# A hybrid decoder block: the order of work around the two halves of the attention values

## The chip, the core and the metric

The kernel runs on one core of a Trainium2 chip. The core has a matrix engine (TensorE, "PE"; its weight loads are listed apart as "PEld"), a vector engine (VectorE, "DVE"), an activation engine (ScalarE, "ACT"), a general-purpose engine (GpSimd, "POOL") and a queue engine (SyncE, "SP") that issues most of the transfers. Each engine works through its own instructions in the order in which they were laid down, and waits on semaphores for the others. The metric is device time in microseconds (us) of one execution; the median of three runs before the change is 1088.16 us (1085.83 to 1088.22).

## The reference, cut to what matters

```python
xn = rmsnorm(h, norm_mix_g)
proj = xn @ w_in                      # 1024 tokens x 2568 columns
q, k, v = ...                         # 512 columns each, 8 heads of 64
log_f = log_sigmoid(proj[..., 2560:] + b_forget)       # 8 columns
att = forgetting_attention(q, k, v, log_f)             # logits + c_i - c_k, c = cumsum(log_f)
uv = gelu(proj[..., 1536:2560])       # u and vg, 512 columns each
vg = rmsnorm over groups of 64, times v_gain
sg = u * (tril(w_s) @ vg per chunk of 128 tokens + b_s)
h = h + concat(att, sg) @ w_out
h = h + conv_ffn(rmsnorm(h), w_up, conv_w, conv_b, w_down)
return rmsnorm(h, norm_final_g)
```

`rmsnorm` divides by the root of the mean square plus 1e-6. All arrays are float32. The projection `proj` is what the change is about; the attention, the output projection and the feed-forward part are left as they are.

## The kernel before, in words

**Arithmetic.** Every float32 operand of a large product is split into a high part (a cast to the fp32r type, mostly on ACT) and a low part (the difference, mostly on DVE), and each product is three matmuls (high times high, high times low, low times high). `split_w` (L152), `own` (L206), `hl_of` (L212) and `tsplit` (L246) do this. The weight splits go through a ring of six buffers (`ring`, tags `wy` x2 and `whl` x4). The products are done in a Strassen form: the input is cut into quarters (x11, x12, x21, x22), the weights into A11, A12, A21, A22; seven products with the operands B11, B21, T2, T3, T1, T4 and B22 replace eight. S1 to S4 are sums of weight quarters. A product is `tprod`/`tmul` (L253) where the tokens are the stationary side, `product` (L420) for queries and keys, 12 matmuls of 512 columns each.

**Stages before the attention, in program order.**

1. Loads (L221 to L242) on SP, in the order in which they are written: x11, x21, x12, the weights of the low value half `wl`, `wl3`, then x22, then the gate's remaining weights `gb`.
2. B11 and B21 products for the gate's `uv` columns; then `values_low(0..3)` (L287), the low half of the values, which also carries the 8 forget columns; between them `t2_of` makes the T2 operand and `hl_of("T2", j, ...)` splits it. From L271 to L316 ACT and DVE are held to the program's order by a chain (`Line.on`).
3. The T2, T3, T1, T4 and B22 products for `uv` (L330 to L395). `sum23(k)` makes the weight sums S3 and S2, `sum4(k)` makes S4, and L353 adds the halves of the `gb` tiles; all of these adds are on DVE. The token norm `rstd1` is made from `xtok` (L363 to L368). Gelu follows as the results come.
4. The upper half of the values (L397 to L407), 96 matmuls of 264 columns; its weights `wh` are loaded into `pt` tiles, the last two late. `keep` stores a half's result in DRAM, and keeps the forget columns in `zf`.
5. Queries and keys: `Weights(0)` (L458), `q1` and `q2`, the last gelu of `ut[1]`, `scale_row` (a PE transpose of `rstd1`, a DVE copy, a write and a broadcast read by ACT's queue, giving the row `rb`), then four steps `qk_step(i)`. Each has the products S2, S3, (A12), S1, A22, the next step's A11, and S4; `nxt_of(i)` does the next step's loads, splits and, on POOL, sums (L447 to L455). `emit` (L528) scales and splits a result and stores it.
6. Mixed into stage 5: `gate_part` (L539) squares and reduces the gate per group of 64 and, on the second call for a half, takes the root and multiplies: for the upper half ahead of step 0, for the lower half in steps 0 and 1. `forget_sums` (L492) makes the log-sigmoid, the four small matmuls with the triangle and the ones (L509, L510), the running sums, and returns `turn` (L517), which transposes and stores.
7. The second value quarters (L637 to L813): `VH` and `VL` are accumulated in PSUM banks from `w0` and `wvr`; `gate_split` (L643) splits the normed gate; `kept(hf)` (L666) reloads a stored half and evacuates it; then `spatial` (L704), chained again on ACT and DVE: it splits the spatial weights, evacuates all eight blocks of `VH` and `VL` with `evac_v`, and runs the eight groups of the spatial product, each in a PSUM bank that DVE and ACT then read.

**What sets the order.** Outside the chained parts a planner lays down each engine's order by its own estimate of when an instruction will be ready, with the program's order as priority; `after(later, earlier)` fixes the order of two instructions on one engine. Tiles with one tag share a fixed number of buffers (`BUFS`, L87: for example `pt` 3, `G` 4, `gg` 2, `t01` 1), so that a new tile waits until an old one's last reader is done.

Of the kernel before, what the change touches and what calls it, by code (L numbers as in the profile page):

```python
# [8 lines left out]
F32 = mybir.dt.float32  # L9
# [56 lines left out]
def block_kernel(ctx: ExitStack, tc: tile.TileContext, xT, xtok, wuv, wv0, wv1, wqk, cpk, bfv,  # L66
# [161 lines left out]
    for k in range(4):  # L228
        load_x("x12", k, k, 1)
    wl = sb("A", [P, 3, 2, 264])  # L230
# [5 lines left out]
    for k in range(4):  # L236
        load_x("x22", k, 4 + k, 1)
# [94 lines left out]
    for k in range(4):  # L332
        tmul(S, tsplit(s2[k]), "T2", k, True)
        sum4(k)
        if k < 2:
            sum23(k + 2)
# [15 lines left out]
    for w in gb:  # L352
        dve.tensor_tensor(out=w[:, 0, :], in0=w[:, 0, :], in1=w[:, 1, :], op=ALU.add)  # L353
# [14 lines left out]
    dve.reciprocal(rstd1, rstd1)  # L368

# [26 lines left out]

    S = [sbank() for _ in range(4)]  # L397
    for k in range(4):
        if k > 1:
            t = sb("pt", [P, 2, 264])  # L400
            sp.dma_start(out=t, in_=wv0[k])
            wh.append(t)
        t = wh[k]
        pool.tensor_tensor(out=t[:, 1, :], in0=t[:, 0, :], in1=t[:, 1, :], op=ALU.add)
        tmul(half(S), tsplit(t[:, 0, :], n=264), "T3", k, True)
        tmul(half(S), tsplit(t[:, 1, :], n=264), "B22", k, False)
    keep(S, 1)  # L407

    rb = sb("t01", [P, 1024])

    def scale_row():
        pst = sbank()
        pe.transpose(pst[0:8, 0:P], rstd1, ident)
        rbt = sb("pt", [8, P])
        dve.tensor_copy(rbt, pst[0:8, 0:P])
        act.dma_start(out=rbd, in_=rbt)
        act.dma_start(out=rb, in_=rbd.rearrange("a b -> (a b)").unsqueeze(0).to_broadcast((P, 1024)))

# [38 lines left out]

    W = [Weights(0)]  # L458
    W[0].split("A11", "A12")
    W[0].sums()  # L460
    W[0].last_sum()
    xu = {}
# [11 lines left out]
    for m in range(4):  # L474
# [1174 lines left out]
```

## Time and profile before

| quantity | value |
|---|---|
| median of three runs | 1088.16 us |
| the profiled execution, its own device time | 1087.45 us |
| its span in the trace | 1085.7 us |
| mean granted clock of PE | 0.993 |
| PE busy | 1054.0 us, 97% |
| DVE busy | 892.8 us, 82% |
| ACT busy | 570.7 us, 53% |
| POOL busy | 236.4 us, 22% |
| DMA, mean over the span | 143 GB/s |

The trace's views are read like this. The timeline lists instructions in order of time: start, duration, engine, line, operation, output and inputs by the program's names, a count where equal ones are merged, and in brackets the idle time before it with what ended it. Most lines of DVE and ACT read L44 or L51, which are the lines of the `Line` helper that records them; they are told apart by their tiles. The view by stretches gives each engine's busy time between two moments, then PE's granted clock, the DMA share and GB/s. Matmul ends are modelled, so a start is a better measure than a duration.

### The profile page before, as it was taken

Reading aid. Unit: us, or ns where it says so; the run is one execution under the profiler, and the core shown is the slowest. Engines: PE = TensorE matmul, PEld = TensorE weight load, DVE = VectorE, ACT = ScalarE, POOL = GpSimd, SP = SyncE. Lnnn points to the kernel's source line nnn. Section 1 sums busy time; section 2 is a strip of 40 time slices with the busy share of each in tenths; the row PEclk is TensorE's granted clock in tenths of the full one; section 3 lists DMA queues with packets and bytes.
Section 4 is the critical chain, followed back from the end, with each engine's and each line's share of the span. In section 5 each row is a group of like instructions: output and inputs, shape, how many; then the busy total and the mean of one; then the engine's idle time right before and its main releaser. Section 6 shows DMA issues by size and latency. Waiting matters only on the chain.

```text
span 1085.7 us, 14637 instructions
## 1 busy us (share of the span) xinstructions
PE 1054.0 (97%) x5157; PEld 884.1 (81%) x5157; DVE 892.8 (82%) x1301; ACT 570.7 (53%) x1015; POOL 236.4 (22%) x177
## 2 busy tenths in 40 slices
PE   9999799979999999999999999999999999999997
PEld 6878677868889888887888888888888888888886
DVE  6993698867778877999899998989988775898774
ACT  6656534545767674754344444445444444454653
POOL 0010243340122353035334333233332000000000
PEclk9999899999999999999999999999999999999999
DMA  9152156845564454322243523323231899433442
GB/s 332 52 185 77 59 137 166 210 153 152 176 180 146 137 194 141 112 98 97 78 165 119 176 95 126 116 68 127 97 107 40 281 329 319 136 98 97 136 127 96
DMA packets 66160, 155.78 MB, mean 143 GB/s; under 512 B 7996, under 2 KB 8724, under 8 KB 66088
## 3 DMA queue, kind: packets, MB, share of 16 engines
q1 hardware_dynamic: 65656, 154.30, 44.4%
q8 instruction: 40, 0.66, 0.3%
q10 hardware_dynamic: 432, 0.57, 0.2%
q14 instruction: 32, 0.26, 0.1%
HBM read 111.96 MB, written 42.87 MB: 143 GB/s over the span
## 4 chain that ended last, share of the span: by engine, by line
PE 74%; DVE 5%; ACT 1%; issue 1%; DMA 0%; DVEq 0%; ACTq 0%; SPq 0%
PE k L1499 19%; PE qa L1241 11%; PE qc L1241 10%; PE qd L1241 10%; PE qb L1241 5%; PE pb L938 3%; PE pb L919 2%; PE pl L879 2%; PE pl L880 2%; PE ps L259 1%; PE pf L963 1%; PE pf L965 1%; PE pf L964 1%; PE pb L1152 1%; PE pb L1151 1%
## 5 line engine op out<-in xcount | busy, mean ns | idle before, releaser
L1499 PE MATMUL k<-whb,wha 128*128 128x512 f32 x924 | 209.8, 389 | 0.0
L1499 PEld LDWEIGHTS k<-whb,wha 128*128 128x128 f32 x924 | 173.4, 188 | 36.2 <-DVE wha L161 0.2
L1241 PE MATMUL qc<-xT,whb 128*128 128x512 f32 x540 | 129.9, 389 | 0.5 <-DVE u L1352 0.5
L1241 PE MATMUL qa<-xB,wha 128*128 128x512 f32 x528 | 127.2, 390 | 0.0
L1241 PEld LDWEIGHTS qc<-xT,whb 128*128 128x128 f32 x540 | 101.2, 188 | 22.1 <-DVE u L1352 0.9
L1241 PEld LDWEIGHTS qa<-xB,wha 128*128 128x128 f32 x528 | 98.8, 188 | 20.8 <-DVE wha L161 0.4
L155 ACT CAST wha<-sg 128x512 fp32r<-128x512 f32 x77 | 47.8, 623 | 96.8 <-PE k L1499 86.2
L155 ACT CAST whb<-sg 128x512 fp32r<-128x512 f32 x82 | 50.5, 617 | 87.3 <-PE qc L1241 68.9
L161 DVE TENSOR_TENSOR wha<-sg,wha 128x512 fp32r<-128x512 f32 x77 | 52.8, 688 | 41.5 <-ACT wha L155 41.3
L920 ACT CAST pt<-pb 128x512 fp32r<-128x512 f32 (+1 forms) x80 | 42.2, 545 | 43.0 <-PE pb L919 34.4
L1241 PE MATMUL qd<-xB,whb 128*128 128x512 f32 x264 | 63.9, 390 | 0.1
L1241 PE MATMUL qd<-xT,whb 128*128 128x512 f32 x264 | 63.6, 389 | 0.0
L161 DVE TENSOR_TENSOR whb<-sg,whb 128x512 fp32r<-128x512 f32 x82 | 57.8, 705 | 4.4 <-ACT whb L155 4.3
L1241 PE MATMUL qb<-xT,whb 128*128 128x512 f32 x252 | 60.9, 389 | 0.0
L1128 POOL TENSOR_TENSOR sg<-raw 128x512 f32<-128x512 f32 x20 | 30.4, 1518 | 136.1 <-DVE whb L161 79.9
L921 DVE TENSOR_TENSOR pt<-pb,pt 128x512 fp32r<-128x512 f32 (+1 forms) x80 | 48.8, 634 | 12.0 <-ACT pt L920 10.9
L1241 PEld LDWEIGHTS qd<-xB,whb 128*128 128x128 f32 x264 | 49.5, 188 | 10.8 <-DVE h L1360 0.5
L1241 PEld LDWEIGHTS qd<-xT,whb 128*128 128x128 f32 x264 | 49.6, 188 | 10.3
L1241 PEld LDWEIGHTS qb<-xT,whb 128*128 128x128 f32 x252 | 47.3, 188 | 9.8
L938 PE MATMUL pb<-pt,V 128*128 128x256 f32 x320 | 52.1, 287 | 0.3 <-DVE pt L921 0.2
L1131 POOL TENSOR_TENSOR sg<-sg,raw 128x512 f32<-128x512 f32 x20 | 33.3, 1666 | 64.2 <-DVE whb L161 64.2
L1129 POOL TENSOR_TENSOR sg<-sg,raw 128x512 f32<-128x512 f32 x20 | 34.9, 1747 | 50.7 <-issue 47.0
(405 smaller groups left out, 2302.9 us busy)
## 6 DMA issues: line engine op xcount, KB each, us to landing
raw<-wup SPq DMA_DIRECT2D x44, 512.0 KB
sg<-hx SPq DMA_DIRECT2D x77, 256.0 KB
hx<-hs SPq DMA_DIRECT2D x44, 256.0 KB
hx<-ca SPq DMA_DIRECT2D x35, 256.0 KB
xT<-wdn SPq DMA_DIRECT2D x28, 256.0 KB
x<-kd SPq DMA_DIRECT2D x24, 256.0 KB
raw<-wqk SPq DMA_DIRECT2D x8, 512.0 KB
qd<-G SPq DMA_DIRECT2D x16, 256.0 KB
```

The lines of the kernel that those rows point to most:

```text
L155: act.copy(h, src)
L161: return eng.tensor_tensor(out=l, in0=src, in1=f32(h), op=ALU.subtract)
L879: seq(pe.matmul(ps[:, c:e], A[:, qs], B[:, c:e], start=True, stop=False))
L880: seq(pe.matmul(ps[:, c:e], A2[:, qs], B2[:, c:e], start=False, stop=True))
L920: casts.append(act.copy(pt[:, 0, 0:w], ptr[:, 0:w]))
L921: los.append(dve.tensor_tensor(out=pt[:, 1, 0:w], in0=ptr[:, 0:w], in1=f32(pt[:, 0, 0:w]), op=ALU.subtract))
L938: seq(pe.matmul(po[0][:, oo:oo + n], lhs, pt[:, s, o:o + n], start=(k == 0 and s == 0), stop=(s == 1 and half)))
L1128: pool.tensor_tensor(out=s[0], in0=a21, in1=a22, op=ALU.add)
L1129: pool.tensor_tensor(out=s[1], in0=s[0], in1=a11, op=ALU.add)
L1131: pool.tensor_tensor(out=s[3], in0=s[1], in1=a12, op=ALU.add)
L1241: pe.matmul(ps, w[:, wi, ks], xb[:, xi, k, :], start=(first and n == 0), stop=(n == 11), skip_group_check=True)
L1499: pe.matmul(banks[bk + m], xh[:, xi, ms], wh[:, wi, :], start=(first and p_ == 0 and n == 0), stop=(p_ == NP - 1 and n == 2), skip_group_c ...
```

## The change

It alters the program's order in stages 1 to 7, and moves some work between engines:

- x22 is loaded ahead of `wl` and `wl3`. In the chained part both halves of T2 are made and split ahead of `values_low(2)`, and the sums into `ut[0]` stand ahead of `values_low(3)`.
- `sum4` and the adds on the `gb` tiles go from DVE to POOL, the latter ordered behind the last `sum4`.
- `rstd1` is written to DRAM by ACT's queue right after it is made, in transposed order, and read back as the row `rb` by SP; `scale_row` is gone.
- All four `wh` loads go into two `G` tiles and stand behind the T4 product.
- `gate_part` only squares and reduces; a new `gate_norm` takes one root and one reciprocal for both halves and then multiplies. The upper half's parts come ahead of the upper values, the rest behind them. The W[0] splits and sums, and the last sums and gelu of `ut[1]`, come between and behind the upper values.
- `forget_sums` is a generator in three pieces: the log-sigmoid ahead of step 0, the small matmuls and running sums behind step 0's S1 product, the transpose and store behind its S4 product.
- `gate_split(0)` follows `gate_split(1)`. The four `VL` blocks are evacuated right after the `VL` product, `kept(1)` follows, both ahead of the `VH` products; `spatial` evacuates only the four `VH` blocks.

The core of the diff:

```diff
+    for k in range(4):
+        load_x("x22", k, 4 + k, 1)
     wl = sb("A", [P, 3, 2, 264])
...
     values_low(1)
+    t2_of(1)
     hl_of("T2", 0, tmp[0][1])
+    hl_of("T2", 1, tmp[1][1])
     values_low(2)
-    t2_of(1)
-    values_low(3)
     for m in range(4):
         dve.tensor_tensor(out=ut[0][:, m, :], in0=S[m], in1=vgt[0][:, m, :], op=ALU.add)
-    hl_of("T2", 1, tmp[1][1])
+    values_low(3)
...
     def sum4(k):
         a12 = ua[k][:, 1, :]
-        dve.tensor_tensor(out=a12, in0=s2[k], in1=a12, op=ALU.add)
+        return pool.tensor_tensor(out=a12, in0=s2[k], in1=a12, op=ALU.add)
...
     for w in gb:
-        dve.tensor_tensor(out=w[:, 0, :], in0=w[:, 0, :], in1=w[:, 1, :], op=ALU.add)
+        after(tc, pool.tensor_tensor(out=w[:, 0, :], in0=w[:, 0, :], in1=w[:, 1, :], op=ALU.add), s4)
...
     dve.reciprocal(rstd1, rstd1)
+    rb = sb("t01", [P, 1024])
+    act.dma_start(out=rbd.rearrange("a p -> p a"), in_=rstd1)
+    sp.dma_start(out=rb, in_=rbd.rearrange("a b -> (a b)").unsqueeze(0).to_broadcast((P, 1024)))
...
+    tprod(S, lambda k: gb[k][:, 1, :], "T4", False)
     wh = []
-    for k in range(2):
-        t = sb("pt", [P, 2, 264])
-        sp.dma_start(out=t, in_=wv0[k])
-        wh.append(t)
-    tprod(S, lambda k: gb[k][:, 1, :], "T4", False)
+    for ks in (range(3), (3,)):
+        t = sb("G", [P, len(ks), 2, 264])
+        for j, k in enumerate(ks):
+            sp.dma_start(out=t[:, j], in_=wv0[k])
+            wh.append(t[:, j])
...
+    def gate_part(hf, t):
+        sq = sb("pt", [P, 2, 512])
+        act.activation(sq, vgt[hf][:, t:t + 2, :], AF.Square)
+        r = gms[:, hf * 32 + t * 8:hf * 32 + t * 8 + 16]
+        dve.tensor_reduce(out=r, in_=sq.rearrange("p t (g d) -> p (t g) d", d=64), axis=AX.X, op=ALU.add)
+    def gate_norm():
+        act.activation(gms, gms, AF.Sqrt, bias=eps[:, 0:1], scale=1.0 / 64)
+        dve.reciprocal(gms, gms)
+        for hf in (1, 0):
+            for t in (0, 2):
+                v3 = vgt[hf][:, t:t + 2, :].rearrange("p t (g d) -> p (t g) d", d=64)
+                r = gms[:, hf * 32 + t * 8:hf * 32 + t * 8 + 16]
+                dve.tensor_tensor(out=v3, in0=v3, in1=r.unsqueeze(2).to_broadcast((P, 16, 64)), op=ALU.mult)
+    gate_part(1, 0)
+    gate_part(1, 2)
+    S = [sbank() for _ in range(4)]
+    def values_high(k):
+        t = wh[k]
+        pool.tensor_tensor(out=t[:, 1, :], in0=t[:, 0, :], in1=t[:, 1, :], op=ALU.add)
+        tmul(half(S), tsplit(t[:, 0, :], n=264), "T3", k, True)
+        tmul(half(S), tsplit(t[:, 1, :], n=264), "B22", k, False)
+    values_high(0)
+    values_high(1)
     W = [Weights(0)]
-    W[0].split("A11", "A12")
+    W[0].split("A11")
+    values_high(2)
+    W[0].split("A12")
     W[0].sums()
     W[0].last_sum()
+    values_high(3)
+    keep(S, 1)
+    for m in range(4):
+        dve.tensor_tensor(out=ut[1][:, m, :], in0=B[m], in1=ut[1][:, m, :], op=ALU.subtract)
+        gelu(ut[1][:, m, :], 4 + m)
+    gate_part(0, 0)
+    gate_part(0, 2)
+    gate_norm()
...
         dve.tensor_tensor(out=ll, in0=z, in1=f32(lh), op=ALU.subtract)
+        yield
+        ps = sbank()
...
+        yield
+        pe.transpose(ps[0:64, 192:320], z, ident)
...
-        if i < 2:
-            gate_part(0, 2 * i)
+        if i == 0:
+            next(fsum)
...
         product(qd_, w.w["S4"], "B22", False)
         if i == 0:
-            turn()
+            next(fsum)
...
     W[0].split("S2", "S3")
-    gate_part(1, 0)
-    gate_part(1, 2)
-    turn = forget_sums(*fg)
+    fsum = forget_sums(*fg)
+    next(fsum)
...
     gate_split(1)
+    gate_split(0)
...
-        for tt in range(8):
-            evac_v(tt, 1, vbank(tt))
+        for m in range(4):
+            evac_v(4 + m, 1, VH[m])
...
         tmul(VL, a1[k], "B11", k, False)
+    for m in range(4):
+        evac_v(m, 1, VL[m])
+    kept(1)
     for k in range(4):
         tmul(VH, tsplit(wvr[k][:, 1, :], n=256), "B22", k, False)
-    gate_split(0)
-    kept(1)
```

More of the change, by code (lines that the diff above doesn't have):

```diff
@@ L333, in block_kernel @@
         tmul(S, tsplit(s2[k]), "T2", k, True)
-        sum4(k)
+        s4 = sum4(k)
         if k < 2:
@@ L395, in block_kernel @@
         gelu(vgt[0][:, m, :], m)
[L397 to L417, printed above, removed]
     def product(ps, w, n, first):
@@ L515, in forget_sums @@
         dve.tensor_tensor(out=v3(z), in0=v3(ps[:, 64:128]), in1=run, op=ALU.add)
[L517 to L523 removed]
+        yield
+        pe.transpose(ps[0:64, 192:320], z, ident)
+        rows = c[0:64, 272:400]
+        act.activation(rows, ps[0:64, 192:320], AF.Copy, scale=-1.0)
+        sp.dma_start(out=ncr.rearrange("h (t p) -> (h t) p", p=P), in_=rows)
+        yield
     fg = forget()
```

28 lines of the change are left out of this document (1 added, 27 removed).

## The prediction

> **What bounds the kernel now.** I read the page's busy shares first, then the busy time of each engine in chosen stretches, then TensorE's (PE's) timeline between them, and last the timelines of the engine named as the releaser of each gap.
>
> ```profile
> span 1085.7 us, 14637 instructions
> PE 1054.0 (97%) x5157; PEld 884.1 (81%) x5157; DVE 892.8 (82%) x1301; ACT 570.7 (53%) x1015; POOL 236.4 (22%) x177
> ```
> PE is idle for 1085.7 - 1054.0 = 31.7 us in all. An order of work can win back that, and the slow clock after each gap, no more. The stretches (columns: busy time of PE, PEld, DVE, ACT, POOL with counts, granted clock, DMA share, GB/s):
> ```profile
> 35.57:55.19 19.62, 16.39 (x88) 13.65 (x86) 19.62 (x32) 11.86 (x24) 0.00 (x0) 1.00 0.15 54
> 112.10:146.85 34.75, 26.06 (x104) 20.32 (x104) 28.70 (x46) 19.35 (x35) 12.61 (x8) 0.90 0.23 72
> 146.85:202.14 55.29, 54.33 (x238) 44.71 (x239) 49.10 (x66) 22.20 (x41) 17.40 (x11) 1.00 0.67 177
> 226.37:242.56 16.19, 10.00 (x51) 8.02 (x49) 11.87 (x20) 9.19 (x22) 9.85 (x13) 0.89 0.52 150
> ```
> Three places lose time: the third Strassen product of the value halves (T3), where VectorE (DVE) is busy without a break; the first query/key step, where PE is idle for 34.75 - 26.06 = 8.7 us; and the spatial product, idle for 6.2. The later query/key steps (third row) lose only 1.0. PE's timeline shows the gaps, with the releaser in brackets:
> ```profile
> 50.83 1.20 PE L259 MATMUL pb<-whl,x 128*128 128x512 f32 x4
> 55.93 9.17 PE L259 MATMUL pb<-whl,x 128*128 128x512 f32 x32 [3.90 <-DVE whl L44]
> 64.94 2.88 PE L259 MATMUL pb<-wy,x 128*128 128x512 f32 x12
> ...
> 115.23 2.88 PE L425 MATMUL qa<-x,whl 128*128 128x512 f32 x12
> 117.95 2.88 PE L425 MATMUL qb<-H,wy 128*128 128x512 f32 x12
> 126.98 0.39 PE L509 MATMUL ps<-gg 128*128 128x64 f32 x1 [6.16 <-DVE gg L44]
> ...
> 146.85 2.56 PE L425 MATMUL qb<-H,wy 128*128 128x512 f32 x10 [2.06 <-DVE wy L44]
> ...
> 228.89 0.39 PE L723 MATMUL pb<-H,wy 128*128 128x512 f32 x1
> 234.19 0.80 PE L721 MATMUL pb<-H,wy 128*128 128x512 f32 x1 [4.92 <-ACT pt L51]
> ```
> A product of 12 matmuls takes 117.95 - 115.23 = 2.72 us, 0.227 each. The 32 matmuls behind the first gap take 64.94 - 55.93 = 9.01 instead of 7.26: a gap of this size also costs about **1.75 us of slow clock**. The granted clocks of 0.90 and 0.89 in the other two places say the same.
>
> **Part 1: the early order and the sums on GpSimd (the T3 gap).** Eight adds leave DVE: four of sum4, four on the `gb` tiles. These are their rows between 35.5 and 55.2:
> ```profile
> L44 DVE TENSOR_TENSOR raw<-gg,raw 128x512 f32<-128x512 f32 x4 | 2.7, 684 | 0.0
> L44 DVE TENSOR_TENSOR G<-G 128x512 f32<-128x512 f32 x4 | 2.6, 683 | 0.0
> ```
> Issued back to back they overlap a little; two neighbours start 38.58 - 37.98 = 0.6 apart:
> ```profile
> 37.98 0.68 DVE L44 TENSOR_TENSOR raw<-gg,raw 128x512 f32<-128x512 f32 x1
> 38.58 0.69 DVE L44 TENSOR_TENSOR whl<-gg,whl 128x512 fp32r<-128x512 f32 x1
> ```
> Removed: 8 x 0.6 = **4.8 us**. What they cost on GpSimd (POOL) is read where POOL adds tiles of the same size today, first with DVE idle, then with DVE wanting two SBUF operands at the same moment:
> ```profile
> 112.85 1.29 POOL L447 TENSOR_TENSOR raw<-raw,raw 128x512 f32<-128x512 f32 x1 [13.11 <-DVE whl L44]
> 139.56 1.62 POOL L447 TENSOR_TENSOR raw<-raw,raw 128x512 f32<-128x512 f32 x1 [20.64 <-ACT gg L44]
> 141.26 1.62 POOL L448 TENSOR_TENSOR gg<-raw,raw 128x512 f32<-128x512 f32 x1
> ...
> 139.95 3.48 DVE L44 TENSOR_TENSOR whl<-raw,whl 128x512 fp32r<-128x512 f32 x2
> ```
> Beside them two DVE operations take 3.48 us, 1.74 each for 0.6 of work: the two engines take turns, and each POOL add takes 1.74 - 0.6 = **1.15 us from DVE**. Everything DVE does between 35 and 55 (sums, weight splits, the T3 and B22 operands) has two SBUF operands, and DVE has no idle time there that would hide it. So eight adds cost 8 x 1.15 = 9.2 and save 4.8. The bounds are 0 (all fall into DVE's waits) and 9.2 (all collide); the upper is the nearer row, since DVE stands at 19.62 of 19.62, and I take it.
>
> [...]
>
> Against this stands a gain before 35.57. The x22 loads move ahead of the `wl` loads, and both T2 operands ahead of values_low(2):
> ```profile
> GB/s 332 52 185 77 59 137 166 210 153 152 176 180 146 137 194 141 112 98 97 78 165 119 176 95 126 116 68 127 97 107 40 281 329 319 136 98 97 136 127 96
> x<-xT SPq DMA_DIRECT2D x4, 256.0 KB
> ...
> 19.48 0.73 ACT L51 CAST whl<-A 128x264 fp32r<-128x264 f32 x2 [0.84 <-DMA A<-wv]
> ...
> ...
> 28.80 0.43 DVE L51 TENSOR_TENSOR wy<-A,wy 128x264 fp32r<-128x264 f32 x1 [1.70 <-ACT wy L51]
> ```
> Four loads of 256 KB at the first slice's 332 GB/s move the first `wl` landing from 19.5 to about 22.6 (an estimate from these rows); values_low(0) isn't needed until PE ends the B21 product, some 5 us after that, which hides it; a landing later than that would cost one for one. In return DVE doesn't sit 1.70 us before values_low(2), but works on the T2 operands; small waits for ScalarE (ACT) remain. Gain 1.4 us, bounds 0 and 2.8 (a wait of the same size again elsewhere). The T3 split thus starts 9.2 - 4.8 - 1.4 = **3.0 us later** than 55.19, and the gap grows from 3.9 to about 6.9; bounds -5.65 (gap and slow clock gone) and +4.4. What is late next is T1, whose operands DVE makes in the same order, so the delay is carried on as a whole. Putting sum4(k) on POOL also makes the write of the next `s2` wait for it (two `gg` buffers); at 1.74 us a turn that stays inside a T2 product of 2.7 us.
>
> **Part 2: gate's norm and the upper values.** Squares, reductions and multiplications for both halves move to the B22 and values_high products, around 95 to 113. There is room:
> ```profile
> 80.00:100.00 20.00, 20.00 (x90) 16.57 (x89) 7.81 (x16) 15.00 (x26) 0.76 (x1) 1.00 0.37 127
> 100.00:120.00 20.00, 19.98 (x134) 18.11 (x133) 8.15 (x13) 7.99 (x22) 6.00 (x4) 1.00 0.07 27
> ...
> L44 DVE TENSOR_REDUCE gms<-pt x4: 1203/1220/1221, 121.4 to 149.1; 128x16 f32<-128x1024 f32 x4
> L44 DVE TENSOR_TENSOR G<-G,gms x4: 1211/1222/1715, 129.0 to 154.6; 128x1024 f32<-128x1024 f32 x4
> ```
> DVE gets 4 x 1.2 + 4 x 1.2 = 9.8 us and a reciprocal in 40 us that hold 16 us of work; ACT gets four squares and one table load. PE (20.00 of 20.00) hides it all; without that cover it would be those 9.8 us. The `wh` tiles move from `pt` to `G`, whose buffers come free as T4's weights are split, before B22, and all four loads are then in time; POOL's W[0] sums move from 113 into values_high. I put Part 2 at 0 by itself. Its worth is that the 9.8 us are gone from 121 to 156, where DVE set PE's pace.
>
> **Part 3: the forget chain in three pieces.** Today PE's queue holds L509 ahead of the S3 product and waits 6.16 us for it, though S3 was split. What ends that wait is the end of the chain of sigmoid's logarithm, which runs between squares and table loads:
> ```profile
> 126.65 0.19 DVE L44 CAST gg<-gg 128x64 fp32r<-128x64 f32 x1
> ...
> 138.75 0.68 DVE L44 TENSOR_TENSOR whl<-raw,whl 128x512 fp32r<-128x512 f32 x1
> ...
> 145.05 1.75 DVE L44 TENSOR_TENSOR wy<-gg,wy 128x512 fp32r<-128x512 f32 x1
> ```
> After the change the triangle product is written behind the S1 product, 3 x 2.72 us later in PE's queue (qb, qc, qd), and the chain starts without squares in front of it: about 118 against a need at 126. Then the next late thing would be W[1]'s S2: its A11 split comes at 138.75, behind the keys' sum on a full DVE, then POOL makes the sums, and the S2 split of 145.05 is what PE waits for (2.06 us). With 6 to 7 us less on DVE here the A11 split can stand where the later steps have it, ahead of the keys.
>
> The price of the stretch 112.10 to 146.85: 8 products and two matmuls are 98 x 0.227 = 22.2 us, small matmuls and transposes at most 2.1 (PE's 26.06 less 22.2 leaves 3.9, of which 1.75 is slow clock), so the loss is 34.75 - 22.2 - 2.1 = **10.5 us**. Bounds of the gain: 0 and 12.2 (8.7 of idle and 3.5 by the clock of 0.90). I take 10.5; the clean third row of the stretches, with the same products, shows what such a step does with DVE less full.
>
> **Part 4: the row of scales by DMA.** A PE transpose, a DVE copy and an ACT-issued pair go; ACT now writes `rstd1` straight into DRAM in 1024 pieces of 4 bytes, and SP reads it back, so SP's queue waits for that write with the `wh` or W loads possibly behind it.
> ```profile
> q10 hardware_dynamic: 432, 0.57, 0.2%
> ...
> 85.31 0.30 ACT L44 ACTIVATE rstd<-ss,eps 128x8 f32<-128x8 f32 x1
> ...
> 133.98 0.69 DVE L44 SCALAR_TENSOR_TENSOR G<-G,t 128x512 f32<-128x512 f32 x1
> ```
> A packet of that queue took 0.002 x 16 x 1085.7 / 432 = 0.08 us. Over 16 engines 1024 pieces are 5 us, on one engine 82 us. The row is known by 85.6 + 3 and first used (133.98) at about 134 + 3 - 7.9 = 129, so some 40 us hide it. I take 5 us, cost 0; beyond 40 it costs one for one.
>
> **Part 5: early evacuations.** PE's gap of 4.92 before 234.19 is a PSUM bank that ACT frees only after eight evacuations, with four slow ones of kept(1) between them:
> ```profile
> 222.25 1.22 DVE L51 TENSOR_TENSOR wy<-pt,wy 128x1024 fp32r<-128x1024 f32 x1 [1.96 <-PE ps L259]
> 226.23 4.17 DVE L44 SCALAR_TENSOR_TENSOR V<-whl,rstd,V 128x256 fp32r<-128x256 f32 x4
> ...
> 233.67 1.65 ACT L51 ACTIVATE pt<-pb,cp 128x256 f32<-128x256 f32 x4 [0.94 <-DVE A L51]
> ```
> Four evacuations (VL) and kept(1) move ahead of the VH products, into DVE waits like the 1.96 us; four (VH) stay, at about 0.45 each on DVE and ACT in turn. PE ends VH at 226.4, they end near 228.6, the first bank is free at 229.3, when PE wants it. Saved: 4.92 + 1.75 = 6.7, less 0.8 for small waits = **5.9**; bounds 0 (kept(1) still in the way) and 6.7. kept(1) now takes a `wy` buffer that the second spatial weight needs; its release, two pairs of evacuations after the VL product, comes about 2 us before the weight is needed.
>
> **Sum.** +3.0 - 10.5 - 5.9 = -13.4. The profiled execution took 1087.45 (span 1085.7 and 1.75 around it), 0.7 below the median of 1088.16: 1087.45 - 13.4 = 1074.05, and on the median 1074.8. I say **1074.5**.
>
> **Rivals.** (a) The moved adds fall beside DVE without cost: the T3 gap closes, -5.65 in place of +3.0: 1066. For it: DVE's own waits on ACT could take some turns; against: 19.62 of 19.62. (b) PE's queue keeps one in-order wait in the first step, on the triangle product or on S2, because the planner places instructions by its own estimate: 6.16 + 1.75 = 7.9 back: 1082.5. For it: that is just what L509 shows today. (c) Nothing gained: DVE paces these stretches (28.70 of 34.75 busy), its total stays, and the gaps only move: 1088. Against: the stretches 80 to 120 have the room. (d) Slower: the row's write runs on one engine, 82 us, past the 40 that hide it: DVE's queue stands 42 us at the first query scaling, and PE behind it: 1074.5 + 42 = 1117. It decides from 40 us on and makes the kernel slower from 40 + 13.4, some 54. For it: 4 bytes a piece, and SP waits behind it; against: the packet row spread over 16 engines.
>
> **How the numbers follow.** Forecast 0.44, (a) 0.16, (b) 0.20, (c) 0.07, (d) and other losses 0.13. The forecast's own range is 1070 to 1079; the 8 in 10 take in (a) and (b) with the bounds of Part 5: 1064 to 1084. Changes under 0.3%, 3.3 us, can't be told from none: faster 0.80, same 0.07, slower 0.13.
>
> **What would show it.** T3: DVE operations of 1.7 us beside POOL's adds between 36 and 53, and T3's first long run of matmuls starting near 59 instead of 55.93; if near 52, (a). First step: no PE gap at the triangle product, S1's product ahead of it, and the second step's qb starting about 135 + 3. Spatial: the gap before the fifth group under 1 us. The row: its first use not waiting on a DMA. The prediction is wrong if the time from the first attention head on changes by more than 1 us, or a new PE gap of over 3 us stands in values_high.

## The result and the profile after

The changed kernel takes **1079.51 us** (median of four runs, 1078.43 to 1080.07); the kernel before, run beside it, 1087.05 (1085.83 to 1088.22). The ratio is 0.993, with a 95% interval of 0.9912 to 0.9947: faster by some 7.5 us, where 13.4 were forecast. The profiled execution of the changed kernel is its fastest, 1078.43.

The head of its page, spans and busy times:

```profile
span 1076.7 us, 14627 instructions
PE 1054.3 (98%) x5156; PEld 885.6 (82%) x5156; DVE 888.9 (83%) x1291; ACT 571.8 (53%) x1015; POOL 247.6 (23%) x185
```

PE is busy as long as before; of its 31.7 idle us, 22.4 are left. The view by stretches has the columns of the prediction's. The rows are T3's preparation on DVE; the last twelve matmuls of `uv` and the upper values; the first query/key step; the later steps; the spatial product:

```profile
32.98:55.26 22.28, 18.53 (x108) 16.00 (x107) 21.10 (x23) 10.76 (x23) 14.68 (x8) 0.99 0.06 25
99.41:118.68 19.27, 16.39 (x110) 15.31 (x109) 18.01 (x25) 13.12 (x25) 5.10 (x4) 0.91 0.24 80
118.68:141.00 22.32, 22.32 (x104) 18.42 (x102) 15.04 (x36) 11.62 (x22) 4.73 (x4) 1.00 0.38 121
141.00:195.51 54.51, 54.51 (x242) 45.14 (x241) 45.79 (x61) 23.03 (x40) 17.65 (x12) 1.00 0.62 167
218.92:233.54 14.62, 10.39 (x50) 7.99 (x49) 10.24 (x20) 7.56 (x18) 6.32 (x9) 0.88 0.40 100
```

The first query/key step is now without a gap: 22.32 of 22.32. In its place the upper values have lost time, which before ran at full clock without a gap (the prediction's stretch of 100 to 120): a gap of 2.88 us stands in front of them, and behind it the granted clock is 0.87 (105.17 to 118.68). The spatial product still loses some 4 us. PE's timeline of the changed kernel at these places:

```profile
54.00 0.50 PE L259 MATMUL pb<-whl,x 128*128 128x512 f32 x1 [3.00 <-ACT x L44]
55.99 10.95 PE L259 MATMUL pb<-whl,x 128*128 128x512 f32 x35 [1.48 <-DVE whl L44]
66.77 2.88 PE L259 MATMUL pb<-wy,x 128*128 128x512 f32 x12
69.49 2.88 PE L259 MATMUL ps<-wy,H 128*128 128x512 f32 x12
...
105.17 2.13 PE L259 MATMUL ps<-wy,x 128*128 128x264 f32 x9 [2.88 <-DVE A L44]
...
118.68 1.55 PE L406 MATMUL qa<-V,whl 128*128 128x512 f32 x6
...
221.96 1.21 PE L722 MATMUL pb<-H,wy 128*128 128x512 f32 x4 [1.04 <-DVE wy L51]
225.70 0.79 PE L720 MATMUL pb<-H,wy 128*128 128x512 f32 x1 [2.53 <-ACT pt L51]
```

From starts like these, in both traces, comes the account (us, between the first matmuls of the products named):

| from, to | before | after | difference |
|---|---|---|---|
| start, T2 product | 39.72 | 39.97 | +0.25 |
| T2, T1 product | 27.94 | 29.52 | +1.58 |
| T1, first query product | 44.44 | 49.19 | **+4.75** |
| first query product, S3 of the second step | 37.15 | 25.15 | **-12.00** |
| S3 of the second step, second value quarters | 52.89 | 51.68 | -1.21 |
| second value quarters, spatial product | 24.23 | 23.41 | -0.82 |
| spatial product, first logits | 16.19 | 14.62 | -1.57 |
| first logits, end | 843.14 | 843.16 | 0.02 |

The sum is -9.0, the difference of the two spans.

### The profile page after: what moved, and what is told of

Its sections match the earlier page's. It is cut to its first block, busy times and chain, and to the rows that moved or that the text cites. A ratio compares the mean times of both kernels' runs of the same rounds, so it can differ in the third digit from the quotient of the medians.

```text
span 1076.7 us, 14627 instructions
## 1 busy us (share of the span) xinstructions
PE 1054.3 (98%) x5156; PEld 885.6 (82%) x5156; DVE 888.9 (83%) x1291; ACT 571.8 (53%) x1015; POOL 247.6 (23%) x185
## 4 chain that ended last, share of the span: by engine, by line
PE 84%; DVE 8%; DMA 3%; ACT 3%; issue 2%; SPq 0%; POOL 0%; ACTq 0%; DVEq 0%; POOLq 0%
PE k L1499 19%; PE qa L1241 11%; PE qc L1241 10%; PE qd L1241 10%; PE qb L1241 5%; PE pb L938 3%; PE ps L259 3%; PE pb L919 3%; PE qa L406 2%; PE qc L406 2%; PE qd L406 2%; PE pl L879 2%; PE pl L880 2%; PE pf L963 1%; PE pf L965 1%
```

## The experiments

Every run is compared with the kernel before on the same chip. "To T1", "T1 to query" and "spatial" are the stretches of the account, in the profiled execution of each run.

| run | median, us | ratio to before (95%) | to T1 | T1 to query | spatial |
|---|---|---|---|---|---|
| before | 1087.05 | 1 | 67.66 | 44.44 | 16.19 |
| after | 1079.51 | 0.993 (0.9912 to 0.9947) | 69.49 | 49.19 | 14.62 |
| e1_adds_on_dve | 1073.08 | 0.9862 (0.9842 to 0.9883) | 63.35 | 46.58 | 14.68 |
| e2_gb_adds_late | 1072.71 | 0.9863 (0.9849 to 0.9878) | 61.61 | 50.31 | 14.55 |
| e3_banks_first | 1076.83 | 0.9904 (0.9886 to 0.9922) | 68.94 | 48.61 | 14.66 |
| e4_kept_first | 1076.63 | 0.9895 (0.9878 to 0.9912) | 68.95 | 49.04 | 13.61 |
| e5_forget_whole | 1079.69 | 0.9929 (0.9915 to 0.9944) | 69.35 | 48.77 | 15.37 |
| e7_before_forget_pieces | 1084.42 | 0.997 (0.9959 to 0.9981) | 69.17 | 44.44 | 15.98 |
| e8_banks_before_split | 1075.46 | 0.9883 (0.9866 to 0.9899) | 68.86 | 48.04 | 14.70 |
| e9_spatial_weight_early | 1077.34 | 0.9907 (0.9892 to 0.9921) | 69.39 | 49.20 | 11.67 |
| e10_casts_then_squares | 1072.63 | 0.9863 (0.9848 to 0.9878) | 69.03 | 44.27 | 14.69 |
| b1_all_mended | 1065.09 | 0.9789 (0.9773 to 0.9806) | 61.50 | 48.03 | 11.39 |
| b3_gelus_behind_casts | 1062.41 | 0.9767 (0.9753 to 0.978) | 61.10 | 45.50 | 10.67 |

**e1_adds_on_dve: what do the adds on POOL cost?** The changed kernel with all eight early adds back on DVE, in their places:

```diff
-        return pool.tensor_tensor(out=a12, in0=s2[k], in1=a12, op=ALU.add)
+        return dve.tensor_tensor(out=a12, in0=s2[k], in1=a12, op=ALU.add)
...
-        after(tc, pool.tensor_tensor(out=w[:, 0, :], in0=w[:, 0, :], in1=w[:, 1, :], op=ALU.add), s4)
+        dve.tensor_tensor(out=w[:, 0, :], in0=w[:, 0, :], in1=w[:, 1, :], op=ALU.add)
```

> The changed kernel with the eight adds (four of sum4, four on the gb tiles) back on DVE at their old places. Measured by where things start on PE, since the planner lays later queues anew. If POOL's adds take the turns from DVE that the T3 gap is made of: DVE does the stretch from the first weight sum (32.98) to T3's first split in 19.6 us as before, not in 22.3, T3's long run of matmuls starts near 53.3 instead of 55.99 and T1 near 66.8 instead of 69.49. [...]

The kernel is 6.4 us faster with eight operations more on DVE. In the changed kernel POOL's adds and DVE's operations beside them read:

```profile
35.01 4.66 POOL L328 TENSOR_TENSOR raw<-gg,raw 128x512 f32<-128x512 f32 x2 [33.29 <-DVE gg L44]
...
44.84 6.82 POOL L353 TENSOR_TENSOR G<-G 128x512 f32<-128x512 f32 x4
```
```profile
32.98 1.28 DVE L44 TENSOR_TENSOR raw<-G,raw 128x512 f32<-128x512 f32 x2
...
38.45 1.77 DVE L44 TENSOR_TENSOR gg<-raw,G 128x512 f32<-128x512 f32 x1 [1.18 <-POOL raw L328]
...
47.05 3.47 DVE L44 SCALAR_TENSOR_TENSOR G<-t,g,G 128x512 f32<-128x512 f32 x2
...
55.26 0.68 DVE L44 TENSOR_TENSOR whl<-raw,whl 128x512 fp32r<-128x512 f32 x1
55.86 1.21 DVE L44 TENSOR_TENSOR x<-G,x 128x1024 fp32r<-128x1024 f32 x1
```

and in this run, with the adds on DVE:

```profile
32.87 1.29 DVE L44 TENSOR_TENSOR raw<-G,raw 128x512 f32<-128x512 f32 x2
...
43.82 1.42 DVE L44 SCALAR_TENSOR_TENSOR G<-t,g,G 128x512 f32<-128x512 f32 x2
...
49.54 1.23 DVE L44 TENSOR_TENSOR x<-G,x 128x1024 fp32r<-128x1024 f32 x1
...
52.48 1.90 DVE L44 TENSOR_TENSOR whl<-raw,whl 128x512 fp32r<-128x512 f32 x3
```

The same two operations take 1.42 us here and 3.47 beside POOL. From the first weight sum to T3's split DVE needs 52.48 - 32.87 = 19.61 us with the eight adds, and 55.26 - 32.98 = 22.28 without them. The second stretch is also shorter by one T3 operand (`x<-G`, 1.13 us from start to start), which stands behind the split there. At 0.6 us each the adds are 4.8 us of DVE's work, so each add on POOL took (22.28 - 19.61 + 4.8 + 1.13) / 8 = 1.08 us from DVE, the wait of 1.18 for POOL's result included: more than the add itself. The early order thus gained by itself, and the move to POOL gave it back. T1 came at 63.35, 3.4 us ahead of the 66.8 expected: in this execution, the fastest of its four, the 32 matmuls behind the smaller gap took 60.63 - 53.22 = 7.41 us, 0.23 each, while in the changed kernel the 35 from 55.99 to 66.77 took 10.78, 0.31 each, at a granted clock of 0.73.

**e2_gb_adds_late: the rest of the T3 gap.** As e1, but the four sums for T1's weights stand behind T3's four splits:

```diff
-    for w in gb:
-        after(tc, pool.tensor_tensor(out=w[:, 0, :], in0=w[:, 0, :], in1=w[:, 1, :], op=ALU.add), s4)
-    tprod(S, lambda k: ua[k][:, 0, :], "T3", True)
+    for k in range(4):
+        w = ring()
+        d3 = split_w(ua[k][:, 0, :], (w[:, 0], w[:, 1]))
+        tmul(S, w, "T3", k, True)
+    for w in gb:
+        after(tc, dve.tensor_tensor(out=w[:, 0, :], in0=w[:, 0, :], in1=w[:, 1, :], op=ALU.add), d3)
```

> The changed kernel with the eight early adds on VectorE, as in the run with all of them in their old places, and four of them (the sums of the gate's T1 weights) ordered behind the four T3 splits. Lock theory: T3's first split on VectorE comes about 2.6 us (four adds of 0.65) sooner than in that run, the gap of 1.76 us ahead of T3's main stretch closes, the T1 product starts at about 61.6 us (63.35 less 1.76), and the time is about 1071.3 us. Rival: the adds, now between T3's splits and T1's, delay the first T1 split by as much as they freed; the gap moves to the head of T1, the values' upper half starts as in that run, and the time stays at 1073 us.

The theory is named after the turns of DVE and POOL, as e1 measured them: 3.47 us for two DVE operations beside POOL's adds, 1.42 without. Up to T1 all came as expected: no gap at T3, T1 at 61.61. But the time hardly fell against e1: PE stood 3.61 us in front of the upper values in place of 1.40. PE's timeline of this run:

```profile
98.02 0.60 PE L259 MATMUL ps<-wy,x 128*128 128x264 f32 x3 [3.61 <-DVE A L44]
```

Rival and theory each had half; the loss is not where the rival put it, at T1, but one stage later.

**e3_banks_first and e8_banks_before_split: the gap in front of the upper values.** A bank is the buffer in PSUM in which PE sums up a product. The four differences that write `A` read the last uv product's banks (`ps`), which the upper values need: their first matmul in the changed kernel (105.17) waited 2.88 us, until DVE had done the first of these differences. In the changed kernel DVE's queue holds other work in front of them:

```profile
97.86 2.34 DVE L44 TENSOR_REDUCE gms<-pt 128x16 f32<-128x1024 f32 x2 [2.71 <-ACT pt L44]
...
101.49 2.34 DVE L44 TENSOR_REDUCE gms<-pt 128x16 f32<-128x1024 f32 x2
103.75 0.68 DVE L44 TENSOR_TENSOR whl<-raw,whl 128x512 fp32r<-128x512 f32 x1
104.34 2.48 DVE L44 TENSOR_TENSOR A<-ps,A 128x512 f32<-128x512 f32 x4
```

e3 puts the two later reductions behind the differences. e8 also moves the first query weight's split there:

```diff
+    for m in range(4):
+        d = dve.tensor_tensor(out=ut[1][:, m, :], in0=B[m], in1=ut[1][:, m, :], op=ALU.subtract)
     W = [Weights(0)]
-    W[0].split("A11")
+    W[0].w["A11"] = w = ring()
+    after(tc, split_w(W[0].src["A11"], (w[:, 0], w[:, 1])), d)
...
-    gate_part(0, 0)
-    gate_part(0, 2)
+    for t in (0, 2):
+        after(tc, gate_part(0, t), d)
```

> The changed kernel with the lower half's two reductions ordered behind the four ut[1] differences on DVE. Theory: the new 2.88 us gap before the upper values is four PSUM banks that these differences free, and they stand behind two reductions of 1.2 us in DVE's queue; the gap goes (upper values from 102.2 instead of 105.17) and with it its slow clock, so that the first query product starts near 114 instead of 118.68: -4.7 us, about 1074.8. Rival: DVE has too much to do between 95 and 107 as a whole; then the gap comes back at another instruction and the first query product starts later than 117.

> The changed kernel with VectorE's part of the first query weight's split and the two lower-half reductions ordered behind the four differences that free the upper values' banks. In the run that held back only the reductions, the split's subtraction stood first and waited for a ScalarE cast that stood behind the four squares. Theory, now with that wait taken away: the differences run as soon as the B22 product ends, the gap of 2.88 us ahead of the values' upper half shrinks to under 0.8, the slow-clock stretch behind it goes, the stretch from the T1 product to the first query product falls from 49.2 us to about 45, and the time is about 1075 us (1079.5 less 4.5). Rival: the differences are bound by something else (the gelu of the other half, the squares' own start), the gap stays over 2 us and the time stays at 1077 to 1079.5 us.

e3 gained little: the gap fell only to 2.27 us, because the split (a subtraction that waits for an ACT cast behind four squares) came to stand in front. e8 took this wait away too, and the gap fell to 1.53, with the slow clock behind it as long as before: 116.90 - 103.19 = 13.71 us from the values' first matmul to the query product, in the changed kernel 13.51. In these profiled executions neither stretch reached its mark (48.61 and 48.04 us, for some 45). e8's median of 1075.46 is near the 1075 expected all the same, and e3's is 2.7 us below the changed kernel's; as the profiled executions do not show the gap closed, these times do not speak for the theory. PE's timeline of e8:

```profile
103.19 2.73 PE L259 MATMUL ps<-wy,x 128*128 128x264 f32 x12 [1.53 <-DVE A L44]
...
116.90 2.93 PE L406 MATMUL qa<-V,whl 128*128 128x512 f32 x12
```

In e8 the upper half's reductions still stand in front, and DVE is idle 2.71 us there for ACT's squares.

**e10_casts_then_squares: nothing of the norm in front.** As e8, and ACT's squares are ordered behind the casts of the first four value weights, and all reductions behind the differences:

```diff
-        act.activation(sq, vgt[hf][:, t:t + 2, :], AF.Square)
+        after(tc, act.activation(sq, vgt[hf][:, t:t + 2, :], AF.Square), casts[3])
...
-    gate_part(1, 0)
-    gate_part(1, 2)
+    casts = []
...
+            casts.append(act.copy(w[:, 0], t[:, i, :]))
...
+    for hf in (1, 0):
+        for t in (0, 2):
+            after(tc, gate_part(hf, t), d)
```

> The changed kernel with, besides the order of the run before it (differences ahead of the split and of the lower reductions), the gate's squares on ScalarE ordered behind the casts of the first four value weights and all four reductions on VectorE behind the differences. In that run 1.53 us of the gap was left: VectorE stood 2.71 us idle for the squares, with the upper reductions, the value splits and the differences queued behind them. Theory: with nothing of the gate's norm ahead, each difference runs as soon as its bank of the B22 product is done; the gap falls under 0.5 us, no slow clock follows it (13.7 us from the values' first matmul to the first query product become about 11.8), and from T1 to the first query product it takes about 44.8 us as before the change (44.4), not 48.0; the time is about 1072 us (1075.5 less 3.2). Rival: the casts were bound by the gelus (ScalarE is busy with eight of them until 97.7 us), so the first value split is late all the same, or the norm, now later, holds up the first step: then the gap or a new wait in the first step is over 1.5 us and the time stays at 1075 us.

This hit: 1072.63 us for the 1072 expected. PE's timeline of this run has no gap, and T1 to the query product takes 113.30 - 69.03 = 44.27 us, as before the change:

```profile
101.67 1.61 PE L259 MATMUL ps<-wy,x 128*128 128x264 f32 x12
...
113.30 2.88 PE L406 MATMUL qa<-V,whl 128*128 128x512 f32 x12
...
138.41 2.88 PE L406 MATMUL qc<-x,wy 128*128 128x512 f32 x12
```

S3 of the second step comes 138.41 - 113.30 = 25.11 us after the query product, as in the changed kernel: the later norm costs the first step nothing. The 4.75 us of the account were thus the order of work in two in-order queues, ACT's and DVE's.

**e5_forget_whole and e7_before_forget_pieces: what freed the first step?** e5 puts the forget chain's matmuls back in front of the first step; e7 makes only the three pieces, in the kernel before:

```diff
     fsum = forget_sums(*fg)
     next(fsum)
+    next(fsum)
...
-        if i == 0:
-            next(fsum)
-        elif i == 2:
+        if i == 2:
             gate_gain(1)
```
```diff
+        if i == 0:
+            next(fsum)
         if i < 2:
             gate_part(0, 2 * i)
...
-            turn()
+            next(fsum)
...
-    turn = forget_sums(*fg)
+    fsum = forget_sums(*fg)
+    next(fsum)
```

> The changed kernel with the small forget matmuls back ahead of the first step, so that PE has them in its queue right behind q2; the gate's work stays where the change put it. As the prediction has it (what cost was the place in PE's queue): the wait comes back, some 6 us and 1.75 of slow clock, the second step's S3 product starts 6 to 8 us later than 143.83. Rival (what cost was the gate's squares, reductions and table loads in front of the chain on ACT and DVE): the chain ends at 124.4, PE is there at 124.1, so the step starts within 1 us of 143.83 and the time stays at 1079.5 to 1080.5.

> The kernel before, with one part of the change alone: the forget chain in three pieces, its matmuls behind the first step's S1 product; the gate's norm, the adds, the loads and the evacuations stay as before. The prediction's step for this part says that the place of the forget matmuls in TensorE's queue costs the 6.16 us of the first step: then that wait goes, at most 0.5 us of it remains, and the time is about 1080.5 us (1087.1 less 6 to 7). The rival, from the run that put the matmuls back and lost nothing: what freed the first step is that squares, reductions and table loads no longer stand ahead of the chain, so the pieces alone leave the chain late, the wait moves to the new place of the matmuls or to the second step's inputs, and the time stays within 2 us of 1087.

e5 lost nothing: 1079.69 us. Its triangle matmuls stand in front of S2 and wait 0.20 us:

```profile
123.97 0.27 PE L526 MATMUL ps<-gg 128*128 128x64 f32 x1 [0.20 <-DVE gg L44]
...
143.80 2.88 PE L406 MATMUL qc<-x,wy 128*128 128x512 f32 x12
```

e7 gained 3.4 us by the medians, half of what the prediction's step asked for. The wait at the triangle product shrank from 6.16 to 0.69, and others came up behind it, the longest for the second step's weights. PE's timeline of e7:

```profile
128.50 0.27 PE L509 MATMUL ps<-gg 128*128 128x64 f32 x1 [0.69 <-DVE gg L44]
...
139.82 4.62 PE L425 MATMUL qa<-V,whl 128*128 128x512 f32 x10 [4.46 <-DVE whl L44]
...
149.43 2.88 PE L425 MATMUL qc<-x,wy 128*128 128x512 f32 x12
```

From the query product (113.61) to S3 of the second step it takes 35.82 us, against 37.15 before and 25.15 in the changed kernel. The two stretches behind it are as short as in the changed kernel, though: 201.11 - 149.43 = 51.68 us to the second value quarters (52.89 before) and 224.51 - 201.11 = 23.40 through them (24.23 before). With the work that the change takes away from here out of the way, the place of the matmuls is all but indifferent (e5: 143.80 - 118.12 = 25.68); with that work in the way a better place helps 1.3 us in the step and 2.0 behind it (e7).

The forget chain itself came no earlier in e7: its triangle product starts 128.50 - 113.61 = 14.89 us after the first query product, 126.98 - 112.10 = 14.88 before. DVE's timeline of the kernel before, then of the changed one, shows the chain's first steps:

```profile
113.11 1.12 DVE L44 TENSOR_TENSOR gg<-zf,rstd 128x64 f32<-128x64 f32 x1 [0.34 <-ACT zf L44]
...
120.40 0.21 DVE L44 TENSOR_TENSOR gg<-gg 128x64 f32<-128x64 f32 x1
```
```profile
119.65 0.22 DVE L44 TENSOR_TENSOR gg<-gg 128x64 f32<-128x64 f32 x1
...
124.19 0.20 DVE L44 CAST gg<-gg 128x64 fp32r<-128x64 f32 x1
```

Before, 7.29 us lie between the chain's first two operations, in which DVE's queue holds above all the splits of the first query weights (`W[0]`), which wait for POOL's sums and ACT's casts; in the changed kernel these splits are done, and the second operation follows the first (119.35) after 0.30 us. From the second operation to the cast, where the gate's squares and reductions stood in between, 126.65 - 120.40 = 6.25 us became 124.19 - 119.65 = 4.54. So 7.0 us of what made the chain early lie where the splits of `W[0]` stood, and at most 1.7 where the squares did. No run moves one of the two alone, nor the load of the chain's bias, which also moved (issued at 97.83 instead of 113.41), so their shares in PE's time are not shown.

**e4_kept_first and e9_spatial_weight_early: the spatial gaps.** In the changed kernel ACT works on the spatial weight (`wy<-pt`) and loads a table before it evacuates the kept values (`V<-wy`), which hold the buffer that DVE needs for the weight's low part. ACT's timeline, then DVE's:

```profile
214.76 1.05 ACT L51 CAST wy<-pt 128x1024 fp32r<-128x1024 f32 x1
215.82 1.28 ACT L51 ACT_TABLE_LOAD   x1
...
217.22 1.69 ACT L44 ACTIVATE V<-wy,rstd 128x256 fp32r<-128x256 f32 x4
```
```profile
217.75 2.89 DVE L44 SCALAR_TENSOR_TENSOR V<-wy,rstd,V 128x256 fp32r<-128x256 f32 x4 [2.28 <-ACT V L44]
220.68 1.23 DVE L51 TENSOR_TENSOR wy<-pt,wy 128x1024 fp32r<-128x1024 f32 x1
```

e4 orders ACT's cast of the spatial weight, and the table load behind it, after the kept values' evacuation. e9 loads the kept values into another buffer, so that the second spatial weight has its own early, and puts the last four evacuations behind the fourth spatial product:

```diff
+        kl[:] = [act.activation(v[:, :, 0, :], p3, AF.Copy, scale=rstd1[:, tt:tt + 1])]
...
+        act.last = kl[0]
         act.on = dve.on = True
         split_w(wr, ws)
```
```diff
-        t = ring(F32).rearrange("p a (b c) -> p (a b) c", c=256)
+        if hf:
+            rn[0] += 1
+            t = sb("pt", [P, 4, 256])
...
-        for m in range(4):
-            evac_v(4 + m, 1, VH[m])
...
+            if g == 3:
+                for j in range(4):
+                    evac_v(4 + j, 1, VH[j])
```

> The changed kernel with ACT's cast of the spatial weights and its table load ordered behind kept(1)'s evacuations. Theory: kept(1) holds the wy buffer that the second spatial weight needs, and ACT comes to it only at 217.2; freed earlier, the gaps of 1.04 and 2.53 us in the spatial product and the slow clock behind them go: the first logits start 4 to 5 us earlier against the end of the VH product (218.92 to 233.54 becomes 10 instead of 14.6), about 1075. Rival: the four VH evacuations alone, in ACT's and DVE's chain, hold the banks: only the 1.04 us goes, about 1078.5.

> The changed kernel with the second half of the kept values loaded into another buffer, so that the low part of the spatial weight finds its buffer free while the values' products run, and with the last four evacuations put behind the fourth spatial product. Theory: the chain low part, then evacuations, then bank release made both gaps (1.04 and 2.53 us) and the slow clock behind them; with it cut, no gap over 0.5 us is left and the stretch from the first spatial product to the first logits falls from 14.6 us to about 10.8, the time to about 1075.7 us. Rival: the evictions of the first four spatial products (DVE 0.41, ScalarE 0.41 each) set the pace in place of the evacuations, or the evacuations now hold up the transposes' banks: the stretch stays over 13 us and the time at 1078 us or more.

In e4 neither theory nor rival came out: the first gap fell from 1.04 to 0.42, the second only to 2.08, and the stretch to 13.61 for the 10 expected. (The median, 1076.63, fell by more than this stretch explains.) The weight's low part is still made from 218.00 to 220.13, and four evacuations by ACT and DVE in turn follow before a spatial bank is read. In e9 all 24 spatial matmuls run without a gap, from 219.61 to 225.08, and the stretch shrinks to 11.67; but a new gap of 1.60 stands in front of the second eight transposes, behind the evacuations, and one of 0.90 in the second value quarters (24.18 us in place of 23.41). So 2.2 us came of the 3.8 expected.

**b1_all_mended and b3_gelus_behind_casts: the mended order.** b1 joins e2, e10, e4 and e9's late evacuations, these with their banks in the order 0, 2, 1, 3. b3 moves the lower half's gelus behind the casts of the first four value weights too:

```diff
         gelu(vgt[1][:, m, :], 4 + m)
         dve.tensor_tensor(out=vgt[0][:, m, :], in0=ut[1][:, m, :], in1=S[m], op=ALU.add)
-        gelu(vgt[0][:, m, :], m)
...
     values_high(1)
+    for m in range(4):
+        after(tc, gelu(vgt[0][:, m, :], m), casts[3])
```

> All mended together: the adds on VectorE with the T1 sums behind T3's splits; the gate's norm behind the value casts and the differences; ScalarE's cast of the spatial weight behind the kept values' evacuations, and the last four evacuations behind the fourth spatial product, banks taken in turn. Theory: the parts lie in separate stretches and add up: T1 at 61.6 us, the first query product 44.8 us later at about 106.4 (111.9 in the run with the adds alone mended), the spatial stretch about 12 us in place of 14.6, the first logits at about 218.5 us and the time about 1064 us. Rival: what is gained ahead only makes the next input late (as the 1.76 us gained at T3 were lost ahead of the values): a gap of 1.5 us or more in front of the values or of the first step stays, and the time is about 1068 us.

> The version with all mended, with the gelus of the gate's lower half on ScalarE moved behind the casts of the first four value weights. In that version T1 came at 61.5 us, but 1.85 us of gap stood in front of the values: the casts began at 93.5 us behind eight gelus (5.0 us), which wait for the row sums of x, whose loads do not come sooner when TensorE does; VectorE stood 6.15 us idle for the first cast. Theory: the casts now come 2.5 us sooner (four gelus of 0.63), the differences follow their banks, the gap goes and with it the slow clock behind it (from the values' first matmul to the first query product 13.4 us become 11.7); the first query product comes at about 106.0 us in place of 109.5, the first logits at about 217.7 and the time is about 1061.8 us (1065.1 less 3.3). Rival: the gate's norm, later by the gelus, now holds up the first step or the forget chain, and the time stays within 1 us of 1065.

In b1 the parts did not quite add up: with T1 at 61.5, ACT's gelus, which wait for the row sums of x from the load of `xtok`, came too late for the values. Its ACT, then its PE timeline:

```profile
81.39 1.06 ACT L44 ACTIVATE t<-t 128x1024 f32<-128x1024 f32 x1 [3.03 <-DMA t<-xtok]
...
88.60 5.00 ACT L44 ACTIVATE G<-G,rstd 128x512 f32<-128x512 f32 x8
93.51 0.40 ACT L44 CAST wy<-G 128x264 fp32r<-128x264 f32 x1
```
```profile
96.15 2.79 PE L259 MATMUL ps<-wy,x 128*128 128x264 f32 x12 [1.85 <-DVE A L44]
```

In b3 four of the gelus stand behind the casts (first cast 90.87), and the values follow the last uv product without a gap; one of 0.35 us comes inside them, and the stretch is 45.50 us for 48.03 in b1. Its PE timeline:

```profile
93.75 2.10 PE L259 MATMUL ps<-wy,x 128*128 128x264 f32 x12
...
106.60 2.88 PE L408 MATMUL qa<-V,whl 128*128 128x512 f32 x12
```

1062.41 us (1061.3 to 1062.82) beats the kernel before by 2.3% and the changed kernel by 17.1 us; 1061.8 was expected.

## Why the prediction was right, and where it was wrong

The direction and the range were right: 1079.51 lies within the 1064 to 1084 given for 8 in 10, and just outside the forecast's own 1070 to 1079. In the profiled executions 9.0 us were gained for 13.4 forecast: Part 2 and Part 5 fell short by 4.75 and 3.5, and Parts 1 and 3 came out better by 1.2 and, with the later steps, 2.7. That errors of 8.3 us one way met 3.9 the other way is luck. Two small slips change nothing: 1.74 - 0.6 is 1.14 and not 1.15, and 4 x 1.2 + 4 x 1.2 is 9.6 and not 9.8; and T3 belongs to the gate's `uv` columns, not to the value halves.

**Part 1, forecast +3.0: the price of the adds right, the early order mis-sized.** T3's split came at 55.26, against 55.19 before, not 3.0 later. The adds took 8.6 us from DVE for 4.8 saved, 3.8 net for the 4.4 forecast: 1.08 us each in place of 1.15. But the weight sums start at 32.98 in place of 35.57, so the early order gained 2.6 and not 1.4, and one T3 operand of 1.1 us came to stand behind the split. Of the +1.58 that reached T1, 1.1 is slow clock: 35 matmuls behind the gap took 66.77 - 55.99 = 10.78 us, for 7.94 at full clock, 2.84 lost where 1.75 were before. The rest is more idle time (3.00 + 1.48 us for 3.90). e1 shows the cost: with the adds back on DVE the kernel is 6.4 us faster. Rival (a), adds at no cost, falls. The turns that the prediction read from its row of 3.48 us came again: 3.47 us for two DVE operations on SBUF operands beside POOL's adds, 1.42 without them. In the changed kernel the four differences at 104.34, which read PSUM banks (`A<-ps,A`), took 2.48 us beside POOL's adds at 104.50 and 105.86, and the four at 58.80 (`A<-ps,G`), with POOL idle, 2.47.

**Part 2, forecast 0: this is the step that failed.** The prediction read 20.00 of 20.00 on PE, counted room for 9.8 us on DVE, and put the part at nothing. It cost 4.75 us. The room was there: DVE even stands idle for 2.71 us in front of the first reductions. But the work was laid down in in-order queues in front of the one thing that PE needed: reductions wait for squares, squares for gelus, and the differences that free PE's banks stand behind the reductions. The prediction named "a new PE gap of over 3 us in values_high" as what would make it wrong; the gap is 2.88, and with the clock behind it the price is above that mark. In the profiled executions e3 and e8 took away parts of this order for 0.6 and 1.2 us, e10 all of it for 4.9.

**Part 3, forecast -10.5: the size right, the reason half wrong.** The first step gained 12.0 us, just inside the bound of 12.2, and the later steps 1.2. But the prediction led with the place of L509 in PE's queue, and e5 and e7 show that this place is worth 3.4 us at most: nothing by the medians where the other work is moved as well, and 3.4 where it is not, of which the profiled execution shows 1.3 in the first step, 1.2 in the later steps and 0.8 in the second value quarters. The rest comes of what the prediction named beside it, that the chain starts earlier and DVE has less to do. It named the squares as what stood in front of the chain; the rows show at most 1.7 us where they stood and 7.0 where the splits of `W[0]` stood. Both are moved by Part 2, whose worth the prediction did name, and whose price it did not see. That this work carries the gain follows from e5 and e7 together; which piece of it carries how much stays open.

**Part 4, forecast 0: right.** The write was issued at 86.65, SP's read at 96.51; the first use, at 131.13, follows DVE's operation before it. The 5 us estimated for 1024 pieces may have been up to 9.9; rival (d) would have needed over 40.

**Part 5, forecast -5.9: right place, size off.** From the second value quarters to the logits 2.4 us were gained, of which e7, without this part, shows 1.0 as well (23.40 and 15.98 us), so that only some 1.4 are shown to be its work. The sign that the prediction named, a gap under 1 us before the fifth group, did not come: it is 2.53. The step that failed is the last sentence of that part: that kept(1)'s buffer comes free about 2 us before the spatial weight needs it. ACT had the weight's cast and a table load ahead of kept(1)'s evacuation, and the low part started only at 220.68, which held PE for 1.04 us. The four evacuations behind it held the banks, for 2.53 us. e4 and e9 show both links; with them mended the stretch is 11.39 in b1 and 10.67 in b3.

**Rivals.** (b) did not come: the first step has no in-order wait. (c) has something: a gap did move, to the values. The time from the first logits on is unchanged within 0.02 us.

## What to carry to other kernels

Room on an engine over a stretch says little (Part 2 had it, and cost 4.75 us): what counted here was which instruction of an in-order queue stood in front of the one that frees the bottleneck's buffer, and what that one waited for. Before work is moved into a stretch without gaps, list what it passes in each queue, and put the operations that free banks first (e10: 4.9 us). Here an elementwise add of 0.60 us, moved from VectorE to GpSimd while VectorE worked on two SBUF operands, took 1.08 us from VectorE and was no gain; and when one part of a change gains, undo its parts one by one, for the gain may belong to another part than the one it was made for.

## What the runs showed of the hardware that was not expected

The price of the slow clock is not a function of the gap alone. PE's timeline of e7 at T3, then of e1:

```profile
56.18 10.43 PE L259 MATMUL pb<-whl,x 128*128 128x512 f32 x32 [3.90 <-DVE whl L44]
66.44 2.88 PE L259 MATMUL pb<-wy,x 128*128 128x512 f32 x12
```
```profile
53.22 7.57 PE L259 MATMUL pb<-whl,x 128*128 128x512 f32 x32 [1.76 <-DVE whl L44]
60.63 2.88 PE L259 MATMUL pb<-wy,x 128*128 128x512 f32 x12
```

Behind the same T3 gap of 3.90 us in the same code, 32 matmuls took 9.01 us before (granted clock 0.81) and 66.44 - 56.18 = 10.26 in e7; behind a gap of 1.76 in e1's profiled execution, the fastest of its four, they took 60.63 - 53.22 = 7.41, near the 7.26 that 32 take at the prediction's 0.227 each; and behind one of 1.53 in e8 the upper values took 2.1 us longer (13.71 against e10's 113.30 - 101.67 = 11.63 with no gap). What decides it in a single case is not shown.
